# Half of an output projection as a 2x2 block product with seven products, its weight sums formed by adding DMAs, on one Trainium2 core

## The chip, the cores and the metric

The kernel runs on one core of a Trainium2 chip. The metric is the device time of one execution in microseconds. The kernel before took 701.5 us (median of 3 runs, 701.0 to 701.63).

## The reference

One decoder layer on 512 tokens with 2048 features, in float32. Two branches read one input projection, a gated linear recurrence and a causal latent attention with 8 heads; their 2 x 1024 results are put side by side, projected, gated and added to x.

```python
mod = c_act @ w_ada[l] + b_ada[l]
shift, scale, gate = jnp.split(mod, 3, axis=-1)
h = rms_norm(x) * (1.0 + scale[:, None, :]) + shift[:, None, :]
proj = h @ w_in[l]
xr, gr, qc, kvc, kr, ga = jnp.split(proj, split_points(IN_SPLITS), axis=-1)
...
y = jnp.concatenate([y_rnn, y_att], axis=-1) @ w_out[l]
x = x + gate[:, None, :] * y
```

The change is in the last two lines: `y` is 512 x 2048, `w_out` is 2048 x 2048.

## The kernel before

Float32 operands are each split in two fp32r parts: ScalarE casts the high part, VectorE subtracts it to get the low part. A product then takes three matmuls, high by high, high by low and low by high (`mm3s`, L147, built on the recorder `mm`, L127). Weights arrive in `wraw` by SyncE (`wload`, L200), and `wsplit` (L205) makes `whi` and `wlo` of them: a ScalarE cast and one VectorE subtraction (all VectorE `tensor_tensor` operations are recorded at L120, all `scalar_tensor_tensor` ones at L104, all ScalarE activations at L92). In the last part of the program there are six `wraw`, three `whi` and three `wlo` buffers of 128 x 512.

The results `y` lie with features on the partitions: `yh[k]` and `yl[k]` hold 128 features of all 512 tokens, k = 0 to 7 from the recurrence, 8 to 15 from the attention, one more for each head that ends. In the output projection (`oproj`, L1064) a block of 128 output features ("column" m, 16 of them) is the stationary side: a weight tile of 128 x 512 holds four k tiles of a column and serves 12 matmuls of 512 tokens each. A column needs 48 matmuls. Its end (`ofin`, L1237) multiplies by the gate and adds x in one VectorE operation, and ScalarE's queue stores it.

The attention (`produce` L877, `attend` L1004) runs head by head. In `nope` (L921) q and k are normalised, multiplied by a gain row, transposed and split; in `attend` the scores are scaled by the reciprocal sum `sm` on VectorE (`pr<-pr,sm`, L116). At a head's end VectorE makes `yt`, and from it come `yh` and `yl`. Work that needs no attention is filled in between by `fillers` (L1141), one step at a time, under the quotas of `ticks` (L1206): the end of the input projection, then columns 0 to 5 over k 0 to 7 into `acc`, then columns 6 to 9 as far as k has come.

The gates are vectors: `gload` (L1098) fetches half a row of `w_ada` (512 KB) on ScalarE's queue into one of three tiles, `gate` (L1105) multiplies and sums it on VectorE (`ada`, L291). `paced` (L1131) starts them at step `GSTART` and lets `GRATE` of them go with each step; what is left goes into the final loop. `oload` (L1123) fetches x for two columns at a time.

The order on each engine is made by a scheduler that follows the program's order and its ties (`issue_after`), save that SyncE's order is the written one. Engines work through their own order strictly. The final loop goes through all 16 columns:

```python
    for n, m in enumerate(order):
        if n < 4:
            mm3(ops[m], wh[:, cols(n)], wl[:, cols(n)], yh[15], yl[15], False, True)
        ks = [] if n < 4 else [(15, 16)] if m in half3 else [(12, 16)] if m in half else [(8, 12), (12, 16)]
        if m not in acc and m not in half:
            ks = [(0, 4), (4, 8)] + ks
```

Of the kernel before, what the change touches and what calls it, by code (L numbers as in the profile page):

```python
# [41 lines left out]
GSTART = 20  # L42
# [5 lines left out]
GRATE = 1.1  # L48
# [4 lines left out]
C_BADA, C_CW, C_CB, C_BA, C_BX, C_LAM, C_QA, C_KVA, C_BXS, NVEC = 0, 48, 80, 88, 96, 104, 112, 116, 120, 128  # L53
R_QN, R_KN, R_QR, R_KR, R_IF, R_ID, R_MK, NROW = 0, 128, 256, 320, 384, 416, 544, 672
# [32 lines left out]
def body(ctx, nc, tc, a):  # L87
# [210 lines left out]
    def setup_rope():  # L298
# [43 lines left out]
        ts(row[:, R_QN:R_QN + P], row[:, R_QN:R_QN + P], sm, None, ALU.mult)  # L342
# [534 lines left out]
    def produce(g):  # L877
# [43 lines left out]
        def nope(pb, u, which, grow, dst):  # L921
# [21 lines left out]
            for d in range(2):  # L943
                sl = slice(u * 256, (u + 1) * 256)
                act(dst[d][:, 0, sl], tp[:, d * 256:(d + 1) * 256], AF.Copy)
                tt(dst[d][:, 1, sl], tp[:, d * 256:(d + 1) * 256], dst[d][:, 0, sl].bitcast(F32), ALU.subtract)
# [50 lines left out]
        def qfin(pb, u):  # L997
            fs = [qrope(pb, u), nope(pb, u, 1, R_QN, qT)]
            return fs + [qpe()] if u else fs

        yield from unit("wq", 384, qh, ql, qfin)
        yield from unit("wkv", 512, kvh, kvl, lambda pb, u: [nope(pb, u, 0, R_KN, kT), val(pb, u)])

    def attend(g):  # L1004
        kT, qT, qp, vt4 = grp[g]
        for hd in range(2):
# [3 lines left out]
            def block(i):  # L1010
# [15 lines left out]
                ts(pr[:, :n], pr[:, :n], sm, None, ALU.mult)  # L1026
# [37 lines left out]
    def oproj(m, k0, k1, first, last, kind="oa"):  # L1064
        halves = last and m == order[-1]
# [11 lines left out]
        else:  # L1077
            mm3s(ops[m], wh, wl, xs, first, last or (m == order[-1] and k1 == 12))
            if m == order[-1] and k1 == 12:
                r = xo[m // 2][:, m % 2]  # L1080
                stt(r, ops[m], mod[:, 32 + m:33 + m], r, ALU.mult, ALU.add)
# [11 lines left out]
    order = list(range(NACC, NACC + 4)) + list(range(NACC)) + list(range(NACC + 4, 16))  # L1093
# [4 lines left out]
    def gload():  # L1098
        j, hf = 32 + order[loaded[0] // 2], loaded[0] % 2
# [5 lines left out]
    def gate():  # L1105
        j, hf = 32 + order[gated[0] // 2], gated[0] % 2
# [13 lines left out]
    XRT = FREE[0:5] + [KT[0], KT[1], QT[0]]  # L1120
    xo, nload = {}, [0]

    def oload():  # L1123
        n = nload[0]
        mp = order[2 * n] // 2
        nload[0] += 1
        xo[mp] = bigt(XRT[n], "xo")
        for d in range(2):
            DMA.dma_start(out=xo[mp][:, d], in_=a["x"][2 * mp + d])

    def paced():  # L1131
        st = 0
        for n, _ in enumerate(fillers()):
# [3 lines left out]
            if n in XSTEPS:  # L1137
                oload()
            yield
# [206 lines left out]
```

## Time and profile before

| what | value |
|---|---|
| median of the runs | 701.5 us |
| the profiled execution | 700.74 us |
| its span, first to last instruction | 698.9 us |
| TensorE busy, matmuls | 99%, 3209 |
| VectorE, ScalarE, GpSimd busy | 75%, 53%, 7% |
| moved by DMA | 148.9 MB, mean 213 GB/s |

The page gives the busy time of each engine, the span in 40 slices with the busy tenths of each (a slice is 17.5 us), the DMA queues (q1 is SyncE's, q10 ScalarE's, q0 GpSimd's), the chain of work that ended last, and groups of instructions. A group's row has its line, engine, operation and tiles, then the number of instructions, their busy time, the mean of one in ns, and the idle time ahead of them with what ended it. Time that a DMA takes is counted from its issue to its landing. Matmuls overlap, so a matmul's listed duration is longer than its share of TensorE's time.

### The profile page before, as it was taken

Reading aid. Unit: us, or ns where it says so; the run is one execution under the profiler, and the core shown is the slowest. Engines: PE = TensorE matmul, PEld = TensorE weight load, DVE = VectorE, ACT = ScalarE, POOL = GpSimd, SP = SyncE. Lnnn points to the kernel's source line nnn. Section 1 sums busy time; section 2 is a strip of 40 time slices with the busy share of each in tenths; the row PEclk is TensorE's granted clock in tenths of the full one; section 3 lists DMA queues with packets and bytes.
Section 4 is the critical chain, followed back from the end, with each engine's and each line's share of the span. In section 5 each row is a group of like instructions: output and inputs, shape, how many; then the busy total and the mean of one; then the engine's idle time right before and its main releaser. Section 6 shows DMA issues by size and latency. Waiting matters only on the chain.

```text
span 698.9 us, 9638 instructions
## 1 busy us (share of the span) xinstructions
PE 691.8 (99%) x3209; PEld 570.8 (82%) x3209; DVE 526.9 (75%) x1019; ACT 370.5 (53%) x804; POOL 52.4 (7%) x87
## 2 busy tenths in 40 slices
PE   8999999999999999999999999999999999999998
PEld 4887877888888888887888888888988888788886
DVE  6559998889995999989857568669797886673322
ACT  4674326333442779893475587787767333222220
POOL 1000000000010111012021021002120000000000
PEclk9999999999999999999999999999999999999999
DMA  9978998849987666473443335233463977875320
GB/s 345 408 305 333 386 382 284 313 167 377 330 280 229 207 204 194 132 208 119 152 139 94 102 121 178 84 122 107 142 209 96 329 251 247 303 242 175 106 91 30
DMA packets 57081, 148.90 MB, mean 213 GB/s; under 512 B 6468, under 2 KB 14532, under 8 KB 53064
## 3 DMA queue, kind: packets, MB, share of 16 engines
q1 hardware_dynamic: 45360, 115.25, 46.9%
q10 hardware_dynamic: 7064, 20.98, 9.1%
q0 software_dynamic: 4608, 12.06, 6.1%
q8 instruction: 25, 0.41, 0.3%
q14 instruction: 24, 0.20, 0.1%
HBM read 144.07 MB, written 4.19 MB: 212 GB/s over the span
## 4 chain that ended last, share of the span: by engine, by line
PE 72%; DVE 7%; ACT 3%; issue 2%; DMA 0%; POOL 0%; DVEq 0%; POOLq 0%; ACTq 0%
PE pp L127 26%; PE oa L127 25%; PE uwkv L127 6%; PE uwq L127 5%; PE sc L127 4%; PE op L127 2%; DVE xc L104 1%; PE tp L1030 1%; DVE wlo L120 1%; DVE pj L104 1%; DVE pj L744 1%; PE tq L942 1%; DVE xc L120 1%; ACT pj L92 1%; DVE xs L120 1%
## 5 line engine op out<-in xcount | busy, mean ns | idle before, releaser
L127 PE MATMUL pp<-h,whi 128*128 128x512 f32 x880 | 217.0, 390 | 1.3 <-DVE h L104 1.3
L120 DVE TENSOR_TENSOR wlo<-wraw,whi 128x512 fp32r<-128x512 f32 (+4 forms) x214 | 155.8, 734 | 79.1 <-ACT whi L92 41.4
L92 ACT ACTIVATE whi<-wraw 128x512 fp32r<-128x512 f32 (+3 forms) x190 | 119.5, 634 | 169.1 <-PE oa L127 59.9
L127 PEld LDWEIGHTS pp<-h,whi 128*128 128x128 f32 x880 | 164.6, 188 | 35.8 <-DVE h L104 1.7
L127 PE MATMUL pp<-h,wlo 128*128 128x512 f32 x440 | 116.4, 391 | 0.2 <-DVE wlo L120 0.2
L127 PE MATMUL oa<-yl,whi 128*128 128x512 f32 (+1 forms) x260 | 101.0, 389 | 0.0
L127 PE MATMUL oa<-yh,whi 128*128 128x512 f32 (+1 forms) x260 | 100.0, 390 | 0.1
L127 PEld LDWEIGHTS pp<-h,wlo 128*128 128x128 f32 x440 | 82.1, 188 | 17.2 <-DVE wlo L120 0.6
L291 DVE CUSTOM_DVE_ANT_0 ada<-ada,cb,vec 128x2048 f32<-128x2048 f32 x31 | 72.7, 2345 | 1.9 <-DMA ada<-in_ada 1.9
L127 PE MATMUL oa<-yh,wlo 128*128 128x512 f32 (+1 forms) x260 | 70.8, 389 | 0.0
L127 PEld LDWEIGHTS oa<-yh,whi 128*128 128x128 f32 x260 | 48.7, 188 | 9.9 <-ACT yh L92 0.5
L127 PEld LDWEIGHTS oa<-yl,whi 128*128 128x128 f32 x260 | 48.9, 188 | 9.3
L127 PEld LDWEIGHTS oa<-yh,wlo 128*128 128x128 f32 x260 | 47.8, 188 | 9.5
L92 ACT ACTIVATE pj<-pp 128x512 f32<-128x512 f32 x50 | 29.3, 596 | 21.0 <-PE pp L127 20.5
L127 PE MATMUL pp<-e,whi 128*128 128x512 f32 x136 | 34.4, 393 | 0.0
L221 POOL DMA_DIRECT2D whi<-in_win x24 | 13.1, 547 | 276.0 <-DMA wraw<-in_win 201.0
L127 PEld LDWEIGHTS pp<-e,whi 128*128 128x128 f32 x136 | 25.5, 188 | 5.7 <-issue 0.5
L127 PE MATMUL uwkv<-whi,kvt 128*128 128x512 f32 x80 | 28.4, 397 | 0.0
L251 POOL TENSOR_TENSOR hs<-hs,mhalf 128x4 f32<-128x4 f32 (+1 forms) x20 | 24.6, 1230 | 1.6
L127 PE MATMUL uwq<-whi,kvt 128*128 128x384 f32 x80 | 23.8, 341 | 0.0
L92 ACT ACTIVATE PT<-tp 128x128 f32<-128x128 f32 (+3 forms) x32 | 14.0, 438 | 18.2 <-PE tp L1030 10.9
L92 ACT ACTIVATE yh<-yt 128x512 fp32r<-128x512 f32 x16 | 10.1, 632 | 24.4 <-DVE yt L120 24.3
(211 smaller groups left out, 999.3 us busy)
## 6 DMA issues: line engine op xcount, KB each, us to landing
ada<-in_ada SPq DMA_DIRECT2D x31, 1024.0 KB, 7.8
ada<-in_ada ACTq DMA_DIRECT2D x32, 512.0 KB, 5.4
wraw<-in_wout SPq DMA_DIRECT2D x59, 256.0 KB, 3.0
wraw<-in_win SPq DMA_DIRECT2D x24, 448.0 KB, 4.0
whi<-in_win POOLq DMA_DIRECT2D x24, 448.0 KB, 3.9
wraw<-in_wkv SPq DMA_DIRECT2D x24, 256.0 KB, 2.6
wraw<-in_winc SPq DMA_DIRECT2D x18, 320.0 KB, 5.5
wraw<-in_winsb SPq DMA_DIRECT2D x18, 256.0 KB, 6.4
```

Of the source, the lines that this page charges most:

```text
L92: return A.activation(out=out, in_=in_, func=func, **kw)
L104: return V.scalar_tensor_tensor(out=out, in0=in0, scalar=scalar, in1=in1, op0=op0, op1=op1, **kw)
L120: return V.tensor_tensor(out=o, in0=x, in1=y, op=op)
L127: return PE.matmul(out=out, lhsT=lhsT, rhs=rhs, start=start, stop=stop, **kw)
L221: G.dma_start(out=hi[:, :n], in_=src)
L251: G.tensor_tensor(out=out, in0=out, in1=mhalf[:, :n], op=ALU.pow)
L291: ttr_last[0] = V.tensor_tensor_reduce(out=t, in0=t, in1=cv, op0=ALU.mult, op1=ALU.add, scale=1.0, scalar=vec[:, C_BADA + j:C_BADA + j + 1 ...
L744: V.tensor_tensor_scan(out=r, data0=al, data1=xc, initial=0.0, op0=ALU.mult, op1=ALU.add)
L942: PE.transpose(tp[:, d * 256 + i2 * P:d * 256 + (i2 + 1) * P], kt[:, q * P:(q + 1) * P], ident)
L1030: PE.transpose(tp[:, j * P:(j + 1) * P], pr[:, j * P:(j + 1) * P], ident)
```

## The change

Columns 0 to 7 stay as they were (`NSTD`), with columns 6 and 7 ahead of 0 to 5. Columns 8 to 15, half of the projection, become a block product C = A B with tokens as rows: A is `y` in 2 x 2 blocks of 256 tokens by 1024 features, B the weights in blocks of 1024 by 512 (`wo2`). Now `y` is the stationary side and a weight tile of 128 x 512 (one k tile) is the moving side, for two tiles of 128 tokens: 6 matmuls for each weight tile (`prod_k`). The seven products are

- X = A11 B11, copied negated to `p1`, then X = X + A12 B21, which is C11;
- Z = S1 T1 with S1 = A21 - A22 and T1 = B11 + B12, copied to `q5`;
- V = S2 T2 with S2 = S1 - A11 and T2 = T1 + B22; `u2` = -V + `p1`;
- V = V + S3 T3 with S3 = -(S2 + A22) and T3 = B12 + B22; `u3` = -V + `p1`, and C22 = `q5` + `u3`;
- Z = Z + S4 B22 with S4 = S2 + A12, and C12 = Z + `u2`;
- V = V + A22 T4 with T4 = T2 + B21, and C21 = V - `p1`.

The sums S are made by VectorE in `sch` (128 x 256 at a time, from the high and the low parts) and split again into `sa` or `sb`, 128 x 1024 at a time. T1, T2 and T4 are made one after the other in the tiles `tch`: SyncE loads B11, and DMAs with `accum_op=add` from GpSimd's queue add the others; T3 is made so in `wraw`. The same kind of DMA adds `p1` and `u3`, and adds x to a result `d` before it is stored. Since tokens are now on the partitions, the gate has to be a row: `dg` spreads it on a diagonal, 4 matmuls with ones sum it, ScalarE copies it to `grow`. `acc` is multiplied by the gate early, and x is added to it by a DMA (`rload`).

With this, the gates are needed earlier (`GSTART`, `GRATE`, `gorder`), the silu of c moves up by a column, the gains of q and k go from a VectorE product to the copies behind the transposes, and for the last four heads the scaling by `sm` goes to ScalarE. The core of the diff:

```diff
-GSTART = 20
+GSTART = 18
...
+NSTD = 8
+GRATE = 1.8
...
-            for q in range(4):
-                c = slice(q * P, (q + 1) * P)
-                stt(kt[:, c], kt[:, c], s[:, q:q + 1], row[:, grow:grow + P], ALU.mult, ALU.mult)
+            k3 = kt.rearrange("p (q c) -> p q c", q=4)
+            tt(k3, k3, s.rearrange("p (q o) -> p q o", o=1).broadcast_to([P, 4, P]), ALU.mult)
...
-                ts(pr[:, :n], pr[:, :n], sm, None, ALU.mult)
+                if g < 2:
+                    ts(pr[:, :n], pr[:, :n], sm, None, ALU.mult)
+                else:
+                    act(pr[:, :n], pr[:, :n], AF.Copy, scale=sm)
...
-    order = list(range(NACC, NACC + 4)) + list(range(NACC)) + list(range(NACC + 4, 16))
+    order = list(range(NACC, NSTD)) + list(range(NACC))
+    gorder = order[:2] + list(range(NSTD, 16)) + order[2:]
...
+    def rload():
+        m = resid.pop(0)
+        act(acc[m], acc[m], AF.Copy, scale=mod[:, 32 + m:33 + m])
+        G.dma_start(out=acc[m], in_=a["x"][m], accum_op=ALU.add)
+        res[m] = acc[m]
...
+    def quarter(kb, hf):
+        def at(k, t):
+            c = slice(hf * 256 + t * P, hf * 256 + (t + 1) * P)
+            return yh[kb + k][:, c], yl[kb + k][:, c]
+        return at
+
+    def prod_k(bk, k, wh, wl, stat, first, last):
+        st = [stat(k, t) for t in range(2)]
+        kw = dict(skip_group_check=True)
+        for b, (sh, sl) in zip(bk, st):
+            mm(b, sh, wh[:, :S], first, False, **kw)
+            mm(b, sl, wh[:, :S], False, False, **kw)
+        for b, (sh, sl) in zip(bk, st):
+            mm(b, sh, wl[:, :S], False, last, **kw)
...
+    def s1sum(k):
+        if k % 4 == 0:
+            t = bigt(FREE[k // 4], "sch").rearrange("p (k s) c -> p (k s c)", k=1)
+            sch.append(t.rearrange("p (k c) -> p k c", k=4))
+        S2K.append(sch[-1][:, k % 4])
+        e = pjt(16 + k % 2, F32, "s1t")[:, LOH]
+        with tc.issue_after(wlast[0]):
+            tt(S2K[k], f(yh[k][:, HIH]), f(yh[8 + k][:, HIH]), ALU.subtract)
+        tt(e, f(yl[k][:, HIH]), f(yl[8 + k][:, HIH]), ALU.subtract)
+        tt(S2K[k], S2K[k], e, ALU.add)
+
+    def prod2(k):
+        prod_k(X, k, *wload(a["wo2"][8 + k, 0], S), quarter(8, 0), False, k == 7)
...
+        X.extend(bank("oa", "X") for _ in range(2))
+        for k in range(8):
+            prod_k(X, k, *wload(a["wo2"][k, 0], S), quarter(0, 0), k == 0, k == 7)
+            if k % 2:
+                yield
+        p1.append(bigt(FREE[4], "p1"))
+        for t in range(2):
+            act(p1[0][:, t], X[t], AF.Copy, scale=-1.0)
...
+        for k in range(4):
+            prod2(k)
+            s1sum(k)
+            if k % 2:
+                yield
...
+        for k in range(4, 7):
+            prod2(k)
+            s1sum(k)
+            if k > 4:
+                yield
...
+    def gaterow(o):
+        ps = bank("z", "g_ps")
+        mm(ps, onesr, dgh[:, o], True, False)
+        mm(ps, onesr, dgl[:, o], False, True)
+        act(grow[:, o], ps, AF.Copy)
+
+    prod2(7)
+    wlast2 = wload(a["wlast"], 2 * P)
+    banks(oa=(6, 5, 6, 0, 1), z=(2, 3), v=(7, 4))
...
+    for k in range(8):
+        DMA.dma_start(out=tch[k], in_=a["wo2"][k, 0])
+        G.dma_start(out=tch[k], in_=a["wo2"][k, 1], accum_op=ALU.add)
...
+    def s2(d):
+        for k in range(8):
+            for y in (yh, yl):
+                tt(S2K[k], S2K[k], f(y[k][:, LOH]), ALU.subtract)
+            if k % 4 == 3:
+                ssplit(d, k // 4, sch[k // 4])
+            yield
...
+    def gen(bk, tiles, stat, first=True, after=None):
+        for k in range(8):
+            wh, wl = tiles(k)
+            prod_k(bk, k, wh, wl, stat, first and k == 0, k == 7)
+            if after is not None:
+                after(k)
+            yield
...
+    def chain_t(o):
+        return lambda k: G.dma_start(out=tch[k], in_=a["wo2"][8 + k, o], accum_op=ALU.add)
+
+    def t3(k):
+        raw = wraw()
+        DMA.dma_start(out=raw[:, :S], in_=a["wo2"][k, 1])
+        G.dma_start(out=raw[:, :S], in_=a["wo2"][8 + k, 1], accum_op=ALU.add)
+        return wsplit(raw, S)
+
+    def tsplit(k):
+        return wsplit(tch[k], S)
...
+    def store(q, t, o, src, g=True):
+        d = src
+        if g:
+            d = pjt((16, 17, 18, 35)[dn[0] % 4], F32, "d")
+            dn[0] += 1
+            tt(d, src, grow[:, o], ALU.mult)
+        tb = 2 * q + t
+        G.dma_start(out=d, in_=a["xtok"][tb][:, 1024 + o * S:1024 + (o + 1) * S], accum_op=ALU.add)
+        G.dma_start(out=a["outt"][tb][:, o * S:(o + 1) * S], in_=d)
...
+    def addp1(u):
+        for t in range(2):
+            act(u[:, t], Vb[t], AF.Copy, scale=-1.0)
+            G.dma_start(out=u[:, t], in_=p1[0][:, t], accum_op=ALU.add)
+            yield
...
+    def c22():
+        for t in range(2):
+            G.dma_start(out=q5[:, t], in_=u3[:, t], accum_op=ALU.add)
+            store(1, t, 1, q5[:, t])
+            yield
...
+    def c21():
+        for t in range(2):
+            tt(u3[:, t], Vb[t], p1[0][:, t], ALU.subtract)
+            store(1, t, 0, u3[:, t])
+            yield
+
+    both(column(order[3]), s1g)
+    for o in range(2):
+        gaterow(o)
+    run(column(order[4]))
+    Z = [bank("z", "Z") for _ in range(2)]
+    SB = shl(1)
+    both(gen(Z, tsplit, sat(SA), True, chain_t(1)), s2(SB))
+    both(column(order[5]), c11())
+    Vb = [bank("v", "V") for _ in range(2)]
+    SC = shl(0)
+    both(gen(Vb, tsplit, sat(SB), True, chain_t(0)), evq5(), s3(SC))
+    both(column(order[6]), addp1(u2))
+    SD = shl(1)
+    both(gen(Vb, t3, sat(SC), False), s4(SD))
+    both(gen(Z, lambda k: wload(a["wo2"][8 + k, 1], S), sat(SD), False), addp1(u3), c22())
+    both(gen(Vb, tsplit, quarter(8, 1), False), c12())
+    both(column(order[7]), c21())
```

What that makes of the engines' orders, at three places. On TensorE the end of the program was column after column, 8 matmuls with high weights (`whi`), then 4 with low ones (`wlo`):

```order
L127 MATMUL oa<-yh_4929,whi 128x512
L127 MATMUL oa<-yl_4930,whi 128x512
L127 MATMUL oa<-yh_4020,wlo 128x512
L127 MATMUL oa<-yh_4318,wlo 128x512
L127 MATMUL oa<-yh_4628,wlo 128x512
L127 MATMUL oa<-yh_4929,wlo 128x512
L127 MATMUL oa<-yh_5260,whi 128x512
L127 MATMUL oa<-yl_5261,whi 128x512
```

Of the change, at the start of Z's first product, behind the two gate rows (`g_ps`; `oa` is a column, `sa` is S1):

```order
L128 MATMUL oa<-yl_5984,whi 128x512
L128 MATMUL g_ps<-dgh,onesr 128x512
L128 MATMUL g_ps<-dgl,onesr 128x512
L128 MATMUL g_ps<-dgh,onesr 128x512
L128 MATMUL g_ps<-dgl,onesr 128x512
L128 MATMUL oa<-yh_5983,wlo 128x512
L128 MATMUL Z<-whi,sa 128x512 x4
L128 MATMUL Z<-wlo,sa 128x512 x2
```

A column's 12 matmuls on four k tiles have become 6 on one k tile, whose four `whi` ones stand ahead of the two `wlo` ones; columns 3 to 5 and the columns' ends now lie between the products.

On VectorE the final loop had little but weight splits (`wlo`) and column ends (`xo`):

```order
L120 TENSOR_TENSOR wlo<-wraw,whi 128x512 x3
L104 SCALAR_TENSOR_TENSOR xo<-oa,mod,xo 128x512
L120 TENSOR_TENSOR wlo<-wraw,whi 128x512 x4
L104 SCALAR_TENSOR_TENSOR xo<-oa,mod,xo 128x512
L120 TENSOR_TENSOR wlo<-wraw,whi 128x512 x4
```

Of the change, around the start of V's first product (`sch`, `s3t` are sums S, `sb` their low part, `d` a gated result, `tch` a summed weight tile):

```order
L121 TENSOR_TENSOR wlo<-wraw,whi 128x512
L121 TENSOR_TENSOR d<-X,grow 128x512
L121 TENSOR_TENSOR sch<-sch,yl_3223 128x256
L121 TENSOR_TENSOR sb<-sch,sb 128x1024
L121 TENSOR_TENSOR sch<-sch,yl_3288 128x256
L121 TENSOR_TENSOR wlo<-wraw,whi 128x512
L121 TENSOR_TENSOR d<-X,grow 128x512
L121 TENSOR_TENSOR wlo<-tch,whi 128x512
L121 TENSOR_TENSOR s3t<-sch,yh_4002 128x256
L121 TENSOR_TENSOR wlo<-tch,whi 128x512
L121 TENSOR_TENSOR s3t<-sch,yh_4302 128x256
```

Between two weight splits there are now one to four sums, a split of 1024 or a gate product. Further on, ahead of V's last product, the gated C22 (`d<-q`) stands in front of that product's first weight split (`wlo<-tch`):

```order
L121 TENSOR_TENSOR sb<-sch,sb 128x1024
L121 TENSOR_TENSOR wlo<-wraw,whi 128x512 x4
L121 TENSOR_TENSOR d<-q_6259,grow 128x512
L121 TENSOR_TENSOR wlo<-tch,whi 128x512
L121 TENSOR_TENSOR d<-q_6259,grow 128x512
L121 TENSOR_TENSOR wlo<-tch,whi 128x512
L121 TENSOR_TENSOR u_6260<-Z,u_6260 128x512 x2
```

GpSimd had nothing to issue after the attention. Of the change, its queue from the first weight sums on (L1382 is T1, L1433 T2 and T4, L1438 T3, L1453 adds x, L1454 stores, L1471 and L1476 are `u` and `q5`):

```order
L1382 DMA tch<-in_wo 128x512 x8
L1438 DMA wraw<-in_wo 128x512 x2
L1433 DMA tch<-in_wo 128x512 x8
L1453 DMA d<-in_xtok 128x512
L1438 DMA wraw<-in_wo 128x512
L1454 DMA outt<-d 128x512
L1453 DMA d<-in_xtok 128x512
L1433 DMA tch<-in_wo 128x512
L1438 DMA wraw<-in_wo 128x512
L1433 DMA tch<-in_wo 128x512
L1454 DMA outt<-d 128x512
L1433 DMA tch<-in_wo 128x512 x6
```

All of these DMAs stand in one queue, the adds of weights among the stores, which wait for their adds of x.

More of the change, by code (lines that the diff above doesn't have):

```diff
@@ L1064, in oproj @@
     def oproj(m, k0, k1, first, last, kind="oa"):
-        halves = last and m == order[-1]
+        halves = last and m == order[-1] and k1 == 16
         if first or halves:
@@ L1166, in fillers @@
             yield
-        for m in range(NACC, NACC + 4):
+        for m in order[:2]:
             oproj(m, 0, 4, True, False)
@@ new lines, in body @@
+    prod2(7)
+    wlast2 = wload(a["wlast"], 2 * P)
+    banks(oa=(6, 5, 6, 0, 1), z=(2, 3), v=(7, 4))
+    for m in order[:3]:
+        run(column(m))
+    p3ctx.close()
+    tp_ = ctx.enter_context(tc.tile_pool(name="tail", bufs=1))
+    grow = tp_.tile([P, 2, S], F32, name="grow")
+    tch = [bigt(HT[i // 2], "tch") if i % 2 == 0 else None for i in range(8)]
+    tch = [tch[i // 2 * 2][:, i % 2] for i in range(8)]
+    for k in range(8):
+        DMA.dma_start(out=tch[k], in_=a["wo2"][k, 0])
+        G.dma_start(out=tch[k], in_=a["wo2"][k, 1], accum_op=ALU.add)
```

187 lines of the change are left out of this document (133 added, 54 removed).

## The prediction

> **What bounds the kernel now.** I read the page's busy rows first, then TensorE's waits, then the last piece of the chain of waits.
>
> ```profile
> span 698.9 us, 9638 instructions
> PE 691.8 (99%) x3209; PEld 570.8 (82%) x3209; DVE 526.9 (75%) x1019; ACT 370.5 (53%) x804; POOL 52.4 (7%) x87
> ...
> DVE  6559998889995999989857568669797886673322
> ...
> PEclk9999999999999999999999999999999999999999
> ```
> ```profile
> PE pp L127 <- DVE h L104: 1.3, 1, 1.3
> PE pp L127 <- DVE xs L116: 1.1, 1, 1.1
> PE junk_ps L127 <- POOL junk L242: 1.0, 1, 1.0
> PE pp L127 <- DVE wlo L120: 0.2, 1, 0.2
> ```
> ```profile
> 604.61 0.70 DVE yt L120
> ...
> 606.02 89.56 PE oa L127 x405
> ```
>
> TensorE is busy 99% of the span at an undisturbed clock, its listed waits add up to 3.6 us, and none of them lies in the output projection. From the last attention head (its yt starts at 604.61) to the end, the chain is one unbroken row of projection matmuls. So a matmul less is worth its pitch, as long as nobody else becomes late. Those who could are VectorE and the DMAs: light at the end, heavy in slices 31 to 36.
>
> The pitch is read from starts, because the listed durations of pipelined matmuls overlap:
>
> ```profile
> 610.93 0.39 PE L127 MATMUL oa<-yh,whi 128*128 128x512 f32 x1
> ...
> 615.47 0.39 PE L127 MATMUL oa<-yh,whi 128*128 128x512 f32 x1
> ```
> ```profile
> 692.53 0.28 PE L127 MATMUL oa<-yh,whi 128*128 128x256 f32 x1
> 692.64 0.28 PE L127 MATMUL oa<-yl,whi 128*128 128x256 f32 x1
> ```
>
> Between the first two starts lie 20 matmuls, so 4.54 / 20 = 0.227 us for one of 512 columns; 0.12 us for one of 256.
>
> **TensorE: −10.0 us.** Eight block products of 48 matmuls (8 k tiles x 2 token tiles x 3 hi/lo terms) become seven: 48 fewer. The gate as a row on all partitions adds 4. The new matmuls have the old form (a 128x128 weight load, 512 moving columns), so I keep the pitch: 44 x 0.227 = 10.0. By the order, 39 of them go after the last head and 5 before it.
>
> **VectorE beside it.** Weights now serve 6 matmuls a tile, not 12, and the left-hand sums are new. The costs:
>
> ```profile
> L120 DVE TENSOR_TENSOR wlo<-wraw,whi 128x512 fp32r<-128x512 f32 x123 | 83.9, 687 | 51.0 <-ACT whi L92 24.1 <-PE oa L127 22.5 <-PE pp L127 2.4
> L104 DVE SCALAR_TENSOR_TENSOR xo<-oa,mod,xo 128x512 f32<-128x512 f32 x10 | 7.2, 748 | 16.1 <-PE oa L127 16.1
> L120 DVE TENSOR_TENSOR wlo<-wraw,whi 128x1024 fp32r<-128x1024 f32 x5 | 6.1, 1224 | 11.9 <-ACT whi L92 7.8 <-PE pp L127 4.1
> L120 DVE TENSOR_TENSOR gl<-graw,gh 128x256 fp32r<-128x256 f32 x8 | 3.4, 420 | 3.1 <-DMA graw<-in_wrg 3.0
> ```
> ```profile
> 516.34 0.42 DVE L120 TENSOR_TENSOR qT<-tq,qT 128x256 fp32r<-128x256 f32 x1
> 516.67 0.16 DVE L120 TENSOR_TENSOR hs<-hs,rl 128x8 f32<-128x8 f32 x1
> 516.83 0.69 DVE L120 TENSOR_TENSOR wlo<-wraw,whi 128x512 fp32r<-128x512 f32 x1
> 517.43 0.69 DVE L120 TENSOR_TENSOR qo<-qs,hs 128x512 f32<-128x512 f32 x1
> 518.03 0.16 DVE L120 TENSOR_TENSOR hs<-hs,rl 128x4 f32<-128x4 f32 x1
> ```
>
> Back to back, a 512-wide operation takes 0.60 us from start to start and a 256-wide one 0.33, some 0.09 less than listed. From the first weight split of Z's first product to the second sb split, where the fifth k step of Z's second product starts, the order gives VectorE 32 weight splits, 48 sums of 256, 6 splits of 1024, 2 gate products and 3 column ends: 34 x 0.60 + 48 x 0.33 + 6 x 1.14 + 3 x 0.66 = 45.1 us. TensorE has 216 matmuls there, 49.0 us. So the sums hide, with 8% to spare. With listed durations they are 53.3 us, 4.3 too many; I take the pitch, since these rows stand back to back.
>
> Z's start hangs on one VectorE queue: the ends of columns 6, 7, 0 and 1, which wait for TensorE, stand ahead of the last sa split and Z's first weight split. After the last of those four, VectorE needs 0.66 + 1.14 + 0.60 = 2.4 us and TensorE has 11 matmuls, 2.5 us. With the two grow copies that must free Z's banks I charge **+0.5** (between 0 and 1.5).
>
> **The last heads.** The gates move ahead of the last head's end; s1sum, dg and more weight splits come in with them.
>
> ```profile
> 530.71:586.22 55.51, 55.51 (x269) 45.43 (x268) 45.87 (x101) 24.36 (x65) 1.20 (x2) 1.00 0.78 264
> 604.58:695.60 91.02, 90.93 (x411) 75.22 (x410) 39.52 (x60) 20.12 (x32) 0.00 (x0) 1.00 0.43 145
> ```
> ```profile
> L291 DVE CUSTOM_DVE_ANT_0 ada<-ada,cbo,vec 128x1024 f32<-128x1024 f32 x9 | 11.5, 1281 | 2.8 <-DMA ada<-in_ada 2.8
> L291 DVE CUSTOM_DVE_ANT_0 ada<-ada,cbo,modh 128x1024 f32<-128x1024 f32 x9 | 11.5, 1279 | 1.4 <-DMA ada<-in_ada 1.4
> ```
> ```profile
> L116 DVE TENSOR_SCALAR pr<-pr,sm 128x512 f32<-128x512 f32 x8 | 3.9, 485 | 0.3
> L116 DVE TENSOR_SCALAR pr<-pr,sm 128x128 f32<-128x128 f32 x8 | 2.3, 282 | 0.1
> ```
>
> The first window runs from the fifth yt to the seventh; its columns are TensorE, weight loads, VectorE, ScalarE, GpSimd. VectorE works 45.9 of 55.5 us and waits 4.2 more for ada. Between the same two yt the new order has one gate more (+1.2), six 512-wide weight splits more and a 384-wide one less (+3.1), 12 sums of 256 and two operations of 1024 (4.0 + 2.3), and without the eight scalings that go to ScalarE (mean 0.38, less the overlap: −2.4): 54.1, and 58.3 with the waits. TensorE's part there shrinks by 5 matmuls to 54.4. So VectorE could come up to 3.9 us late. A lead of up to three weight buffers (1.4 to 2.7 us each) can swallow that; TensorE shows no wait there today. Ends 0 and 3.9: I take **+1.8**, about the middle.
>
> **The adding DMAs.** 46 of them run near or after the last head, 256 KB each, from GpSimd's queue: 32 weight sums, 6 between results, 8 that add x. None is in this trace. The nearest rows:
>
> ```profile
> q1 hardware_dynamic: 45360, 115.25, 46.9%
> ...
> q0 software_dynamic: 4608, 12.06, 6.1%
> ```
> ```profile
> whi<-in_win POOLq DMA_DIRECT2D x24, 448.0 KB, 3.9
> ...
> out<-xo ACTq DMA_DIRECT2D x15, 256.0 KB, 2.8
> ...
> gh<-in_wrg POOLq DMA_DIRECT2D x8, 128.0 KB, 3.2
> ```
>
> In landing time I take 3.5 us, between the two GpSimd rows. In occupancy, the queues' shares give 115.25 MB / (0.469 x 698.9) = 352 GB/s on SyncE's queue, 0.75 us for 256 KB, and 283 GB/s on GpSimd's, 0.93 us. Ends for an adding one: 0.75, and 1.5 if it counts as two of SyncE's transfers. I take 0.93, the row of its own queue. Between the last head and V's last product lie 287 matmuls, 65 us; tch can load some 7 us earlier, when SyncE's queue comes to it. In these 72 us about 36 plain and 40 adding ones are due: 27 + 37 = 64 us. They fit.
>
> The shortest cover is VectorE's queue ahead of V's last product: d<-q stands in front of its first weight split. From V's second end: a copy (0.6), two adds in sequence with their issue (2 x 4.0), the gate product and the split (1.2), 9.8 us, under Z's 48 remaining matmuls, 10.9 us. Cost nothing; if an add takes 1 us longer, the cover is gone and 0.9 is lost.
>
> The end:
>
> ```profile
> 694.92 0.64 PE L127 MATMUL oa<-yh,wlo 128*128 128x256 f32 x4
> 695.60 0.48 DVE L104 SCALAR_TENSOR_TENSOR xo<-oa,mod,xo 128x256 f32<-128x256 f32 x1 [0.95 <-PE oa L127]
> ```
>
> Now 3.3 us pass from 695.60 to the end. After V's last matmul the column that remains takes 12 x 0.227 + 24 x 0.12 = 5.6, plus 3.3: 8.9. The other branch needs two subtractions and two gate products (2.4), an add with issue (4.0), a store (2.8) and its issue: 9.4. It ends last: **+0.5** (0 to 3). The Trainium skill (DMA: Bandwidth & Descriptors, Anatomy of one DMA) fits 2.0 us plus the bytes over 436 GB/s to such a transfer, 2.6 us here as an estimate. By that the branch would end before the column and the +0.5 would go; the two landing rows, 3.2 and 3.9, lie above it.
>
> ScalarE, 20.1 of 91.0 us at the end now, stays off the path even doubled. GpSimd stops in its queue at the stores of C11, which wait for their adds of x (about 4 us each), and V's next weight sums stand behind them; those are needed a product later, 11 us. SyncE's eight tch loads stand ahead of the weights of columns 1 and 2 and wait for the K and Q tiles of the last two heads; these are free when the last scores are done, before the last yt, and the weights are needed some 10 us after it. Folding the gains of q and k into copies that are there anyway, and the silu of c one column earlier, get no price: VectorE's idle 25% covers them.
>
> **Sum.** −10.0 + 0.5 + 1.8 + 0.5 = −7.2. The profiled execution took 700.74 us (1.8 beyond its span), so 693.5; the median of the runs is 0.8 above it, 701.5: **694.3 us**.
>
> **Rivals.**
> 1. *The adds fill the DMA engines (slower).* An add reads its destination as well as its source. At 1.5 us each, the DMAs due before V's last product need 27 + 60 = 87 us of 72: t3's weights and then d<-q are late and TensorE waits some 15 us: 709. At 0.93 there are 8 us of room; the room ends at 1.1 us each and the gain at 1.3. For: nothing in the trace shows an add at the price of a copy. Against: the tail's DMA share is 0.43 today, and x and tch load early. Chance 0.2. The Trainium skill (Collectives: The Full Stack, Part 3, on the fold count) says that a reduce step runs at half a copy's rate because the add needs two source reads; no run shown here tests it, and by that rule the sum would be this rival's.
> 2. *VectorE becomes the bound.* If its operations wait on semaphores and keep their listed durations, 4.3 us are lost in the sums and all 3.9 in the heads: −10.0 + 0.5 + 3.9 + 4.3 + 0.5 = −0.8, 700.7. Against: the pitch rows. Chance 0.12.
> 3. *All of it hides.* Without the 1.8 and the 0.5 at Z: −9.5, 692.0. For: no TensorE wait in the heads today at 50 busy or waiting of 55.5. Chance 0.22.
>
> My forecast keeps 0.46. That the change doesn't remove the matmuls can be excluded: the order has 48 fewer in the products.
>
> **Range and chances.** 691.5 (all hidden, the end free too) to 705.0 (half of rival 1's loss): some 0.15 is left out, nearly all above. A measurement of this kernel tells about 0.2% (1.4 us) from no change: faster 0.72 (forecast, rival 3, the better part of an add that costs little over its room), same 0.10 (mostly rival 2), slower 0.18.
>
> **What would show it.** 44 fewer matmuls at 0.227 us in Z, V and X. TensorE's waits: none on wlo from tch or wraw inside Z and V (else rival 2, or rival 1 if ScalarE's whi before them waits for a DMA). The issue rows of tch and wraw from GpSimd near 3.5 us. No VectorE wait over 1 us at d<-q. The end some 9 us after V's last matmul. An add that lands in 5 us or more, or a DMA share of 0.95 between the last head and Z's second product, would make the forecast wrong.

## The result and the profile after

The change makes the kernel slower: 735.88 us (median of 4 runs, 733.24 to 736.89) against 701.25 (700.78 to 701.63), a ratio of 1.0488 with a 95% interval of 1.0457 to 1.052. The profiled execution took 736.89 us, 1.8 beyond its span. Its page, in the form of the page before:

```profile
span 735.1 us, 9800 instructions
...
PE 694.9 (95%) x3165; PEld 566.3 (77%) x3165; DVE 564.3 (77%) x1061; ACT 412.3 (56%) x873; POOL 103.6 (14%) x147
...
PEclk9999999999999999999999999999999999997698
DMA  9978998769886675552533253536549959989775
...
q1 hardware_dynamic: 44784, 113.55, 44.2%
q0 software_dynamic: 12736, 27.79, 17.5%
```

The 44 matmuls are gone (3165 instead of 3209), but TensorE now idles: its busy share falls from 99% to 95%, and in the last slices even the granted clock falls. The DMA row stands at 0.8 or more in slices 34 to 37; before, it fell from slice 36 on:

```profile
DMA  9978998849987666473443335233463977875320
```

Which wait of TensorE is new stands in its list of waits (total, times, longest), and behind it in ScalarE's:

```profile
PE V L128 <- ACT whi L93: 20.0, 4, 13.2
PE V L128 <- DVE wlo L121: 1.9, 2, 1.7
PE uwq L128 <- ACT whi L93: 1.9, 1, 1.9
```
```profile
ACT whi L93 <- DMA wraw<-in_wo: 31.6, 5, 15.5
```

V waits for a weight copy, and that copy waits for a DMA into `wraw`: these are T3's tiles, in V's second product. GpSimd's queue in the timeline (start, duration, line, operation; in brackets the idle time ahead and its releaser) shows when their adds (L1438) were issued:

```profile
650.33 0.89 POOL L1438 DMA_DIRECT2D wraw<-in_wo  x1 [0.90 <-issue]
655.54 0.59 POOL L1454 DMA_DIRECT2D outt<-d  x1 [4.32 <-DMA d<-in_xtok]
...
656.75 1.20 POOL L1433 DMA_DIRECT2D tch<-in_wo  x1
657.39 1.47 POOL L1438 DMA_DIRECT2D wraw<-in_wo  x1
664.58 0.87 POOL L1433 DMA_DIRECT2D tch<-in_wo  x1 [5.72 <-DVE sch L121]
665.19 0.83 POOL L1454 DMA_DIRECT2D outt<-d  x1
...
676.39 0.88 POOL L1433 DMA_DIRECT2D tch<-in_wo  x1 [0.62 <-issue]
677.62 0.87 POOL L1471 DMA_DIRECT2D u<-p  x1 [0.36 <-issue]
679.34 0.87 POOL L1438 DMA_DIRECT2D wraw<-in_wo  x1 [0.84 <-issue]
```

The fourth add of T3 goes out at 657.39, the fifth only at 679.34: between them stand a wait of 5.7 us, a store, seven adds of T4 (L1433, 664.58 to 676.39), which is needed two products later, and an add to u2. The stretches of 20 us (columns: the stretch; TensorE, weight loads, VectorE, ScalarE, GpSimd busy; clock, DMA share, GB/s) show the price:

```profile
640.00:660.00 20.00, 20.00 (x88) 16.15 (x87) 17.29 (x35) 10.69 (x18) 8.84 (x11) 1.00 0.90 170
660.00:680.00 20.00, 7.28 (x24) 4.76 (x23) 5.46 (x11) 2.00 (x3) 8.24 (x10) 0.79 1.01 217
680.00:700.00 20.00, 12.14 (x38) 8.35 (x39) 9.25 (x18) 7.28 (x12) 4.42 (x7) 0.70 0.73 149
```

From 660 to 700 TensorE does 62 matmuls where 176 would have fitted at 0.227 us. The DMA engines are full until 680, and once TensorE has idled the granted clock is 0.79 and 0.70. The same four matmuls before and behind a wait show what that costs:

```profile
661.18 1.07 PE L128 MATMUL V<-whi,sa 128*128 128x512 f32 x4
...
668.68 2.07 PE L128 MATMUL V<-whi,sa 128*128 128x512 f32 x4 [4.13 <-ACT whi L93]
```

The next pair of matmuls starts 0.91 us behind the first of these rows and 1.87 behind the second: 0.47 us for a matmul instead of 0.23, at a granted clock of 0.50 from 668.68 to 671.60. Eighteen matmuls went at this pace, 4.3 us more than at 0.227.

To see where the time went, every profiled execution is cut at two marks, the start of the first and of the last yt. The sum of the three pieces is the span.

| kernel | to the first yt | first to last yt | last yt to the end | median of runs |
|---|---|---|---|---|
| before | 425.1 | 179.5 | 94.3 | 701.25 |
| predicted (span 691.7) | 425.1 | 180.2 | 86.4 | 694.3 |
| after | 428.0 | 187.2 | 120.0 | 735.88 |

(The prediction's pieces: +1.8 and 5 matmuls fewer in the heads; 39 matmuls fewer, +0.5 and +0.5 at the end.) Of 43.4 us too many, 33.6 lie behind the last head, 7.0 in the heads and 2.9 at the start. Of the 33.6, TensorE's waits in V are 21.9 and the slower matmuls 4.3; the end behind V's last matmul takes 13.4 us instead of 9.4. A profiled execution can lie over 2 us from the median of its runs (705.82 against 708.38 in e2), so pieces are good to some 2 us.

### The profile page after: what moved, and what is told of

It reads as the page before. It is cut to its first block, busy times and chain, and to the rows that moved or that the text cites. A ratio compares the mean times of both kernels' runs of the same rounds, so it can differ in the third digit from the quotient of the medians.

```text
span 735.1 us, 9800 instructions
## 1 busy us (share of the span) xinstructions
PE 694.9 (95%) x3165; PEld 566.3 (77%) x3165; DVE 564.3 (77%) x1061; ACT 412.3 (56%) x873; POOL 103.6 (14%) x147
## 3 DMA queue, kind: packets, MB, share of 16 engines
q0 software_dynamic: 12736, 27.79, 17.5%
## 4 chain that ended last, share of the span: by engine, by line
PE 63%; DVE 11%; issue 10%; DMA 7%; ACT 4%; POOL 4%; POOLq 0%; SPq 0%; ACTq 0%; DVEq 0%
PE pp L128 35%; PE oa L128 8%; PE uwkv L128 6%; PE uwq L128 5%; DMA wraw<-in_wo 3%; PE sc L128 3%; DVE wlo L121 2%; PE op L128 2%; POOL tch L1433 2%; DMA d<-in_xtok 1%; DVE ada L292 1%; DVE xc L105 1%; PE tp L1034 1%; PE X L128 1%; DVE pj L745 1%
## 5 line engine op out<-in xcount | busy, mean ns | idle before, releaser
L121 DVE TENSOR_TENSOR wlo<-wraw,whi 128x512 fp32r<-128x512 f32 (+5 forms) x216 | 155.8, 730 | 81.6 <-ACT whi L93 56.5
L93 ACT ACTIVATE whi<-wraw 128x512 fp32r<-128x512 f32 (+4 forms) x192 | 119.4, 630 | 147.1 <-PE pp L128 62.7
L128 PE MATMUL oa<-yl,whi 128*128 128x512 f32 (+1 forms) x132 | 50.9, 388 | 1.0 <-DVE yl L121 1.0
L128 PE MATMUL oa<-yh,whi 128*128 128x512 f32 (+1 forms) x132 | 50.7, 388 | 0.3 <-ACT yh L93 0.3
L128 PE MATMUL oa<-yh,wlo 128*128 128x512 f32 (+1 forms) x132 | 36.7, 388 | 0.0
L128 PE MATMUL V<-whi,sa 128*128 128x512 f32 x32 | 12.0, 501 | 20.0 <-ACT whi L93 20.0
L128 PEld LDWEIGHTS oa<-yl,whi 128*128 128x128 f32 x132 | 24.8, 188 | 5.5 <-DVE yl L121 1.2
L128 PEld LDWEIGHTS oa<-yh,whi 128*128 128x128 f32 x132 | 24.8, 189 | 5.2 <-ACT yh L93 0.5
L128 PEld LDWEIGHTS oa<-yh,wlo 128*128 128x128 f32 x132 | 24.0, 188 | 4.5
L93 ACT ACTIVATE whi<-tch 128x512 fp32r<-128x512 f32 x24 | 15.0, 632 | 21.9 <-DVE wlo L121 6.3
```

The costliest lines, as they stand in the source:

```text
L93: return A.activation(out=out, in_=in_, func=func, **kw)
L121: return V.tensor_tensor(out=o, in0=x, in1=y, op=op)
L128: return PE.matmul(out=out, lhsT=lhsT, rhs=rhs, start=start, stop=stop, **kw)
```

## The experiments

Theory A, formed from this: an adding DMA costs the DMA engines twice a copy, so the weight sums are late. Rival B: it is the order and the waits in GpSimd's one queue, at any price. Rival C: VectorE. D and E concern the start and the stretch at 440 us. The pieces of all runs in the table's form:

| run | to the first yt | first to last yt | last yt to the end | median |
|---|---|---|---|---|
| e1_plain_copies | 426.8 | 186.6 | 99.0 | 713.29 |
| e2_no_sums | 427.2 | 184.8 | 92.0 | 708.38 |
| e3_t4_after_t3 | 426.5 | 185.8 | 109.4 | 725.63 |
| e4_late_ones | 425.1 | 185.9 | 122.5 | 733.57 |
| e5_silu_back | 426.4 | 190.4 | 120.0 | 736.61 |
| e6_gpsimd_sums | 427.6 | 187.7 | 129.8 | 746.28 |
| e7_no_adding_dma | 426.1 | 187.7 | 135.4 | 750.51 |
| e8_all_mended | 425.5 | 188.4 | 134.1 | 749.95 |
| e9_sums_free_ends_mended | 425.3 | 187.1 | 87.7 | 701.02 |
| e10_no_x_to_acc | 426.7 | 188.4 | 121.6 | 736.43 |
| e11_mended_on_dma | 426.0 | 187.3 | 100.5 | 715.85 |
| e12_half_gates | 424.8 | 190.5 | 85.2 | 702.36 |
| e13_old_gates | 425.5 | 179.4 | 99.7 | 706.49 |
| e14_only_sums_add | 426.1 | 184.3 | 98.9 | 711.55 |
| e15_t3_own_tiles | 426.3 | 186.9 | 100.3 | 713.25 |
| e16_half_loads | 425.8 | 182.2 | 87.8 | 696.5 |

**Copies in place of the weight sums, and none at all.**

```diff
-        G.dma_start(out=tch[k], in_=a["wo2"][k, 1], accum_op=ALU.add)
+        G.dma_start(out=tch[k], in_=a["wo2"][k, 1])
```

The same in `chain_t` and `t3`; in the second run the three lines are left out.

> The 32 adding DMAs of the weight sums T1 to T4 become copies to the same place in the same queue, so the same number of transfers and waits, without the second read; the products use wrong sums. Theory A (an adding DMA occupies the DMA engines about 1.5 us where a copy of 256 KB takes 0.75): 24 us of DMA time go away, T3's weights come in time, TensorE's 25 us in front of and inside V's second product go; 12 us or so of losses at the start and in the heads stay: 705 to 713. Rival B (the order and the waits in GpSimd's one queue, whatever a transfer costs): T3's weights stay late, 725 to 736.

> The 32 adding DMAs of the weight sums are left out; the products use single blocks for the sums. Theory A and rival B: both lose what makes T3 late, 702 to 712, and within 2 us of the copies under A, over 15 us below them under B. Rival C (VectorE's sums and gates hold up TensorE, with any weights): stays above 715, with TensorE's waits on wlo and on d.

With copies 713.29, ratio to before 1.0165 (1.0148 to 1.0182): 22.6 us less than the change, in the same queue and order. That is 0.3 over A's range and far from B's 725. Without the sums it is 708.38, 1.0096 (1.0075 to 1.0117), 4.9 less again, where A had said up to 2 and B over 15. A is nearer in both. The price stands in the DMA queues: GpSimd's row (packets, MB, share of 16 engines' span) with copies and without any, to be held against the one after (12736, 27.79, 17.5%):

```profile
span 712.3 us, 9800 instructions
...
q0 software_dynamic: 10688, 27.79, 14.3%
```
```profile
span 704.0 us, 9730 instructions
...
q0 software_dynamic: 8128, 19.40, 11.0%
```

17.5% of 735.1 us are 128.6 us, 14.3% of 712.3 are 101.9, 11.0% of 704.0 are 77.4. The 32 adding DMAs took 51.2 us, 1.60 each; the 32 copies 24.4, 0.76 each. The bytes listed are the same, the packets are not: 144 for each adding DMA, 80 for each copy. SyncE's queue took 324.9 us after, 321.2 with the copies and 321.7 without any, so the 51.2 us hide little that a fuller engine adds to other transfers. What the copies don't separate is GpSimd's own pace: it issues a copy in 0.55 us and one behind the other (five in 2.89 us), an adding DMA in 0.88 with pauses of 0.4 to 2 us. Two adds that go out when the engines are less full (a share of 0.60 from 722 on) have no pause (the x2 row at 724.56 below), so the pauses look like the full engines holding the queue back; no run shows that by itself.

**T4 behind T3 in GpSimd's queue.** The eight adds of T4 are written behind V's second product and tied behind T3's last add.

```diff
-    both(gen(Vb, tsplit, sat(SB), True, chain_t(0)), evq5(), s3(SC))
+    both(gen(Vb, tsplit, sat(SB), True), evq5(), s3(SC))
...
+    with tc.issue_after(t3last[0]):
+        for k in range(8):
+            chain_t(0)(k)
```

> T4's eight adds go to GpSimd's queue behind all of T3's, instead of ahead of the last four of them. Theory A: the DMA engines stay as full, a part of the wait moves from V's second product to its third: 722 to 731. Rival B: the idle time in V's second product goes and nothing takes its place: 706 to 716.

725.63 us, 1.0355 (1.0317 to 1.0393): A's range. The order was worth 10 us, and a part of the wait moved to V's third product:

```profile
PE V L128 <- DVE wlo L121: 7.8, 2, 6.6
PE V L128 <- ACT whi L93: 5.6, 2, 4.4
```

The 6.6 us are for a weight split of the third product that stands behind `d<-q`, for which VectorE waits 7.9 us: the adds on u3 and q5 now stand in GpSimd's queue behind T4's eight. So this part is order again, not the engines' time alone; e11 below takes these adds out of the queue, and the wait is gone.

**The start.** `act(onesr, ones, AF.Copy)` becomes `tab(...)`, which ties it behind the last exponential.

> The copy of ones to onesr on ScalarE is tied behind the last exponential, so that it no longer stands ahead of the first silu. Theory D (it costs the start about 2 us by a table load that it draws with it): 733 to 734.5, the first yt at 425 to 426. Otherwise 735 to 737, the first yt at 428.

733.57 us, 1.0467 (1.0451 to 1.0482), 2.3 less than the change. ScalarE's timeline at the start, after and in this run:

```profile
2.61 0.31 ACT L93 ACTIVATE onesr<-ones 128x128 fp32r<-128x128 f32 x1
2.94 1.28 ACT L93 ACT_TABLE_LOAD   x1
4.23 0.63 ACT L93 ACTIVATE c4i<-c4i 4x512 f32<-4x512 f32 x1
```
```profile
1.32 1.28 ACT L93 ACT_TABLE_LOAD   x1 [1.32 <-PEq L1581]
3.25 0.63 ACT L93 ACTIVATE c4i<-c4i 4x512 f32<-4x512 f32 x1 [0.64 <-DMA c4i<-in_c4i]
```

The scheduler had put the copy, which belongs behind the last head and needs nothing, ahead of the silu of c (`c4i`), where it draws in one more table load; the silu starts 1.0 us later. Over all profiled executions the first yt comes at 426.9 on average in the eight with the early copy and at 425.6 in the nine with the late one: 1.3 us, less than the 2.9 of this pair.

**The silu of c back.** `load_c` at column 1, the silu at column 2, `GSTART` 20.

> The silu of c goes back to its old column and the gates start two steps later again (20 instead of 18); their rate stays at 1.8. Theory E (the table load and the two silus, 3.3 us of ScalarE at 440 us, stood ahead of a weight copy and cost TensorE about 3 us): 732.5 to 734. If the late gates then cost as much in the last heads, or if the weight sums are late whatever came before: 735 to 737.

736.61 us: no gain. From the first yt to the fifth it took 105.3 us instead of 110.1, from the fifth to the last 85.1 instead of 77.1. Most of the first gain, 3.4 us, lies ahead of the second yt, where the change had the silu of c and only one gate. What it gave, the later gates took. In the kernel after, this stands ahead of the weight copy for which TensorE (`uwq`, above) waits:

```profile
439.91 1.28 ACT L93 ACT_TABLE_LOAD   x1
441.21 2.01 ACT L93 ACTIVATE cbo<-cbo 128x1024 f32<-128x1024 f32 x2
443.12 0.61 ACT L93 ACTIVATE whi<-wraw 128x512 fp32r<-128x512 f32 x1
```

**The sums on GpSimd.** Each weight sum is made from two plain loads, T4 behind T3 (e6); the adds on results too (e7); with the start and the silu mended (e8).

```diff
+    def gadd(dst, src):
+        add = tp_.tile([P, S], F32, tag="tadd", name="tadd", bufs=4)
+        DMA.dma_start(out=add, in_=src)
+        G.tensor_tensor(out=dst, in0=dst, in1=add, op=ALU.add)
```

> The 32 weight sums are made by additions on GpSimd from two plain loads of SyncE's queue (the second into four tiles of its own), T4 behind T3 as in the run before; the adds on results and x stay adding DMAs. Theory A: the second read goes away, the transfers stay, as with the plain copies: 706 to 714 if an addition on GpSimd takes up to about 1.5 us and VectorE keeps its pace. Rival F (GpSimd's additions are too slow, or slow VectorE down, which has 8% to spare here): 716 to 730. Rival B needs the order only: about 716 to 720, as if half of the copies' gain were the order's.

> As the run of GpSimd's weight sums, and the adds of results and of xtok to d are additions on GpSimd too (xtok loaded ahead by SyncE). The landing of an adding DMA, 4.7 us, goes from the end branch: 3 to 5 us below the run of GpSimd's weight sums if the end of that one is this branch, 702 to 710; no gain if the last column's store ends last.

> All of it: sums and results on GpSimd, the silu at its old column with the gates from step 20, the copy of ones behind the last exponential. If the causes add up (start 2.3, silu 2.5 to 3): 697 to 705, and the first version with a chance to beat the kernel before. If the heads take back what the silu gives: 702 to 708.

746.28, 750.51 and 749.95 us (ratios 1.0648, 1.0708, 1.0706, each within 0.002). Rival F (GpSimd's additions are slow or slow VectorE down) is nearest, and it is worse than it said; the expectations of e7 and e8 failed. GpSimd and VectorE in the run with the weight sums on GpSimd:

```profile
643.31 1.36 POOL L1381 TENSOR_TENSOR tch<-tch,tadd 128x512 f32<-128x512 f32 x1 [2.48 <-issue]
645.63 1.39 POOL L1381 TENSOR_TENSOR tch<-tch,tadd 128x512 f32<-128x512 f32 x1 [0.96 <-DVE wlo L121]
```
```profile
643.10 0.41 DVE L121 TENSOR_TENSOR sch<-sch,yh 128x256 f32<-128x256 f32 x1
643.43 1.51 DVE L121 TENSOR_TENSOR sch<-sch,yl 128x256 f32<-128x256 f32 x1
644.87 0.68 DVE L121 TENSOR_TENSOR wlo<-tch,whi 128x512 fp32r<-128x512 f32 x1
...
645.81 1.76 DVE L121 TENSOR_TENSOR wlo<-tch,whi 128x512 fp32r<-128x512 f32 x1
```

The VectorE operation that starts beside an addition of GpSimd takes 1.1 us longer (1.51 instead of 0.41, 1.76 instead of 0.68), nearly GpSimd's whole 1.4 us. Over the whole run VectorE is busy 590.6 us instead of 564.3, 0.8 for each of the 32 sums, and TensorE waits 17 us behind the last head for what VectorE makes. The Trainium skill (SBUF — State Buffer, Who interferes with whom) says that a VectorE instruction with two SBUF inputs contends with a GpSimd instruction that reads SBUF; these rows agree.

That isn't all. TensorE's longest wait in e6, 8.5 us ahead of a column, is for the column's weights: their loads stand in SyncE's queue behind those of the second addends (`tadd`) and go out at 628.45 instead of 610.62. So e6 to e8 changed SyncE's order too, and don't give GpSimd's additions a price of their own.

**The sums free and both ends mended.** On the run without sums: the late copy, and for the last six token tiles VectorE adds x from tiles loaded ahead, makes u3 and adds q5.

```diff
+            xa = tp_.tile([P, S], F32, tag="xa", name="xa", bufs=4)
+            DMA.dma_start(out=xa, in_=xs)
+            tt(d, d, xa, ALU.add)
...
+                stt(u[:, t], Vb[t], -1.0, p1[0][:, t], ALU.mult, ALU.add)
...
-            G.dma_start(out=q5[:, t], in_=u3[:, t], accum_op=ALU.add)
+            tt(q5[:, t], q5[:, t], u3[:, t], ALU.add)
```

> The weight sums are left out as in the second run (the products use single blocks), and two other terms are mended: the copy of ones behind the last exponential, and the results of the last six token tiles without adding DMAs (VectorE adds x from tiles that SyncE loads ahead, makes u3 in one operation and adds q5). If the terms add up: 708.4 less 2.3 at the start and 3 to 4 in the end branch, 701.5 to 703.5; what then stays above the sum of the matmuls lies at 440 us and in the heads. If VectorE has no room for its 14 operations there: 705 to 709.

701.02 us, 0.9998 (0.9989 to 1.0008), half a us under the range: the terms add up. The end piece falls to 87.7, 1.3 above the predicted 86.4. So with sums for nothing, and the mended ends, the change would gain nothing: its 44 matmuls are spent in the heads. VectorE is full in this run, and behind the last head TensorE waits for it only 0.2 us:

```profile
640.00:660.00 20.00, 20.00 (x90) 16.53 (x89) 19.35 (x39) 10.89 (x17) 3.82 (x5) 1.00 0.58 156
```

**No x to acc.** The adding DMA in `rload` is left out.

> The six adding DMAs that add x to acc are left out (columns 0 to 5 come without x); all else as in the change. If the DMA engines, full from 560 to 580 us, cost the heads their 4 us: 730 to 733.5. If VectorE's queue with the earlier gates does: 735 to 737.

736.43 us, no change: these six don't cost the heads anything.

**Mended, the sums still adding DMAs.** e11 is e3 with the edits of e9; in e14 C11's adds of x and u2's of p1 go to VectorE too; in e15 T3 has four tiles of its own.

```diff
-        if (q, o) == (0, 0):
+        if False:
...
-        raw = wraw()
+        raw = tp_.tile([P, S], F32, tag="t3r", name="t3r", bufs=4) if k % 2 else wraw()
```

> A correct version: T4 behind T3, the copy of ones late, 10 of the adding DMAs on results replaced by VectorE as above, the 32 weight sums still adding DMAs. Theory A: 725.6 less 2.3 at the start, 3 to 4 at the end and some 2 to 5 of the wait in V's second product, for 10 adding DMAs less: 714 to 720. If only the weight sums set the wait: 719 to 722.

> A correct version: as the mended one on DMAs, and also C11's adds of x and u2's of p1 go to VectorE, so that only the 32 weight sums and the six adds to acc are adding DMAs, and GpSimd's queue holds only these and the stores. If the queue's order still cost (T3's fourth add stood behind d and u): 710 to 714. If VectorE, full from 620 to 660 us, has no room for six more operations: 715 to 719.

> As the run just ahead, with four tiles of T3's own besides the six weight buffers, so that its raw loads and adds need not wait until column weights free theirs. If the buffers and the order made T3 late: V's second product waits under 2 us, 703 to 708. If the DMA engines' time for 32 weight sums of 1.5 us sets the pace whatever the order: 710 to 715, DMA share 0.9 or more from 620 to 690 us.

715.85 (1.0199, 1.0163 to 1.0235), 711.55 (1.0151, 1.0136 to 1.0166) and 713.25 (1.0175, 1.0159 to 1.019). Clearing the queue, with four adding DMAs fewer, gave 4.3 us; tiles for T3 gave nothing, they moved the wait to V's first product. e14 stands 10.5 us above e9, which differs by the 32 sums, T4's place and four operations more on VectorE, and its DMA share from 600 to 680 us is 0.97, 1.08, 0.87 and 1.07 (e15: 1.09, 1.01 and 1.04 from 620 on):

```profile
660.00:680.00 20.00, 14.81 (x54) 10.07 (x53) 15.03 (x29) 7.58 (x12) 7.02 (x8) 0.91 1.07 259
```

So what is left goes with the DMA engines' time: neither the cleared queue nor T3's own tiles removed it. That GpSimd's pace has no part in it isn't shown. e14 is the fastest version found with the whole computation, and it doesn't reach the kernel before.

**What costs the heads.** On e9: half of each gate product (e12), that and half of each load of `ada` (e16), or the silu, start and rate of the kernel before (e13).

```diff
-        ttr(gq.pop(0), cb2[hf], j, hf == 0, hf == 1)
+        g_ = gq.pop(0)
+        ttr(g_[:, :, :256], cb2[hf][:, :, :256], j, hf == 0, hf == 1)
...
-        A.dma_start(out=t, in_=a["ada"][j][:, hf * 1024:(hf + 1) * 1024].rearrange("p (k s) -> p k s", k=2))
+        c = a["ada"][j][:, hf * 1024:(hf + 1) * 1024].rearrange("p (k s) -> p k s", k=2)
+        A.dma_start(out=t[:, :, :256], in_=c[:, :, :256])
```

> As the run with the sums left out and both ends mended, and each of the 32 gate products takes only the first half of its elements (128x512 instead of 128x1024; the other half of the sum over c is left out). The loads stay. If VectorE's load by the earlier gates costs the heads: some 20 us of VectorE go between 470 and 600 us, the heads lose at most 1 to 2 us instead of 6, and the time is 695.5 to 698. If the transfers of ada or ScalarE's queue do: 700 to 702.

> As the run with the sums left out and both ends mended, with the silu of c, the gates' start (20) and their rate (1.1) as in the kernel before; some six gates then come behind the last head. If place and rate of the gates were the cause: the 3 us at 440 go and the heads lose 2 to 3 us less, 696 to 699. If the heads take back what the silu gives, as in the fifth run: 700 to 703.

> As the run with half of each gate product, and ada is loaded only for that half (256 KB instead of 512 for each of the 32). Theory H (gates at a rate of 1.8 wait for their loads, and yt and the weight splits stand behind them in VectorE's queue): VectorE's waits for ada nearly go, the heads lose 2 to 3 us instead of 6, 697.5 to 699.5. If the loss is of another kind (the order of ScalarE's copies, say): 701 to 703.

Half the products gave nothing (702.36, against 701.02 in e9), half the loads on top gave 5.9 us: 696.5, 0.9934 (0.9917 to 0.995). From the fifth yt to the last e9 took 78.0 us, e12 81.9 and e16 73.0 (before: 73.9). So it is the transfers of ada at the faster rate, not VectorE's work in the gates. VectorE's waits for ada between 555 and 600 us are in e9, e12 and e16:

```profile
DVE ada L292 <- DMA ada<-in_ada: 4.4, 4, 1.7
```
```profile
DVE ada L292 <- DMA ada<-in_ada: 6.3, 5, 1.7
```
```profile
DVE ada L292 <- DMA ada<-in_ada: 3.7, 1, 3.7
```

Before they are 1.9 us. How they reach TensorE is in e9's timeline. A gate waits for its load, and yt stands directly behind it in VectorE's queue:

```profile
565.85 1.28 DVE L292 CUSTOM_DVE_ANT_0 ada<-ada,cbo,modh 128x1024 f32<-128x1024 f32 x1 [1.69 <-DMA ada<-in_ada]
...
567.07 0.69 DVE L121 TENSOR_TENSOR yt<-op,pj 128x512 f32<-128x512 f32 x1
```
```profile
567.81 0.33 PE L1034 MATMUL tp<-row,pr 128*128 128x128 f32 x1 [2.02 <-DVE yt L121]
```

This is 2.0 of TensorE's 2.6 us of waits in that stretch, and the clock behind it is 0.62 from 567.8 to 572. In e12 a weight split stands behind such a gate (580.90, after 1.42 us) and costs TensorE 1.6. In e16 TensorE works all of the 45 us; its one long wait for ada costs nothing there. So theory H holds for the cause, and these rows show its path.

e13 (706.49) has the heads of before, 179.4 us, and loses more than that behind them:

```profile
PE g_ps L128 <- ACT dgh L93: 4.7, 1, 4.7
PE g_ps L128 <- DVE dgl L121: 3.4, 1, 3.4
```

The row of gates can't be made before the last gates are there. Early gates cost the heads, late ones the sums; both of its expected ranges missed this.

## Why the prediction was wrong, point by point

- **TensorE −10.0.** Right: 44 matmuls fewer, and e9's end piece comes within 1.3 us of the predicted one.
- **VectorE hides the sums of S.** Right, with less to spare than said: 19.35 of 20 us busy in e9, in a stretch where TensorE never idles. Rival 2 falls.
- **Z's start, +0.5.** Right: after, TensorE waits 0.6 us at Z's start (0.4 for grow, 0.2 for the split).
- **The adding DMAs: "I take 0.93, the row of its own queue ... They fit".** This is the step that failed. The term's price is 1.60 us, just over the upper end that I had kept for rival 1, so its sum of 87 us in 72 becomes 91; its 15 us of loss were too small. Rival 1 had the mechanism, and both signs named against the forecast came: a landing over 5 us, and a DMA share of 1.07 from 620 to 640. By the pieces, the second reads, with the longer issue that comes with them, cost 21.0 us (after to e1) and the 32 transfers themselves 7.0 (e1 to e2; 4.9 by the medians), which I had taken for free. GpSimd's order, to which the sum gave no price, made it worse: 10 us went with T4 behind T3. So did the clock, 4.3 us behind the waits. That the queue stops at the stores cost something too (4.3 us in its row, an add of T3 close behind); how much of the 4.3 us of e14 is this and how much its four adding DMAs fewer, stays open. The Trainium skill's rule that I had weighed (Collectives: The Full Stack, Part 3, on the fold count: the add's two source reads halve the rate) is stated there for the steps of a ring; 1.60 against 0.76 agrees with it. The landing of 3.5 us was 5.8 for tch and 6.7 for T3 in a full queue. The Trainium skill's fit (DMA: Bandwidth & Descriptors, Anatomy of one DMA), an estimate of 2.6 us, lies further off.
- **d<-q is covered.** Wrong: from the issue of u's adds (699.29) to d<-q pass 10.0 us where I had 8.0 for the two adds in sequence, and u3's copies came 1.5 us later than I had them. VectorE waited 4.4 us there, TensorE 1.7 behind it.

```profile
709.31 0.69 DVE L121 TENSOR_TENSOR d<-q,grow 128x512 f32<-128x512 f32 x1 [4.41 <-DMA q<-u]
```

- **The end, +0.5.** Mis-sized: 13.4 us from V's last matmul, not 9.4. The last two adds, issued together, free their stores 5 and 7 us later, and the end comes 3.4 us behind the last store's issue:

```profile
724.56 1.85 POOL L1453 DMA_DIRECT2D d<-in_xtok  x2
729.72 0.58 POOL L1454 DMA_DIRECT2D outt<-d  x1 [3.31 <-DMA d<-in_xtok]
731.66 0.57 POOL L1454 DMA_DIRECT2D outt<-d  x1 [1.36 <-DMA d<-in_xtok]
```

  Without adding DMAs on these results 4.3 us go (e2 to e9).
- **The last heads, +1.8.** Right sign, wrong mechanism and size: 7.0 too many. I had counted VectorE's operations; halving its gate work changed nothing. The loads of ada cost about 5 us (e16): VectorE waits for them with yt and weight splits behind it in its queue. And "the silu of c one column earlier gets no price" was wrong: the cover I named was VectorE's idle time, but the silu is ScalarE's, 3.3 us with its table load, and it stood ahead of a weight copy; with it back (e5, e8, e13) the stretch from the first yt to the fifth takes 105.3 us (before 105.6), not 110.1, though the gates start later in these runs too.
- **The start, not in the sum.** One copy more on ScalarE went to the front of the program: 1.3 to 2.3 us, and no term of the sum stood for it.

## What to carry to other kernels

A gain in matmuls has to be paid from the resources of its own stage: count the DMA engines' time there, with an adding DMA at two copies, before VectorE's operations. In an in-order queue an entry that is due later must not stand ahead of one that is due now; look too at what a new order puts last, since here the wait moved with it. An instruction that depends on nothing was put at the front by the scheduler, so look there too.

## What the runs showed of the hardware

- An adding DMA of 256 KB from HBM occupies the DMA engines for 1.60 us (weight sums) or 1.42 (the six of x, from the 17.5% after and the 16.3% of 736.8 us in e10), a copy in the same queue for 0.76.
- GpSimd takes 0.88 us to issue an adding DMA and 0.55 a plain one. In a row of adds at full DMA engines it sits 0.4 to 2 us between two for nothing that the profile shows; a pair late in the program goes out without a pause.
- A single GpSimd addition of 128x512 into `tch` takes 1.26 to 1.42 us (2.0 on average into `wraw`), and a VectorE operation with two SBUF inputs that starts beside it takes 1.1 us longer.
- After TensorE's waits of 4.1 and 13.2 us the granted clock was 0.50 and a matmul took 0.47 us instead of 0.23, so a wait cost more than its length.
